# Attention: GpSimd instead of VectorE makes the low halves of the output projection's weights

## The chip, the cores and the metric

The kernel runs on one core of a Trainium2 chip. A core has five engines with a queue each, and every queue is worked off in order: PE (TensorE, matrix products; its weight loads have a row of their own, PEld), DVE (VectorE), ACT (ScalarE), POOL (GpSimd) and SP, which here only issues transfers. PE writes its products to the PSUM banks; DVE, ACT and POOL work on SBUF, DVE and ACT on PSUM too. The metric is the device time of one execution in microseconds. Three runs of the kernel before gave 622.75, 623.11 and 625.85 us; the median is 623.11.

## The reference, cut to what matters

Two layers on 256 tokens of width 1024, in float32: layer 0 mixes by pooling, layer 1 by attention with a shared K/V. Behind each stands a gated convolution FFN and a gated input embedding. The change lies in the attention of layer 1:

```
def nsa_attention(h, w_in, w_out, cos, sin, kv):
    ...
    proj = h @ w_in                       # queries and gates
    ...                                   # three branches per block of queries: compressed, selected, window
    out = gate0 * o_c + gate1 * o_s + gate2 * o_w
    ...
    o = o.transpose(1, 0, 4, 2, 3, 5).reshape(B, S, N_HEADS * HEAD_DIM)
    return o @ w_out                      # 1024 x 1024: the output projection
```

## The kernel before, in words

The products are taken in fp32r, a rounded float32. To keep float32's accuracy, each operand is split into a high part (rounded to fp32r) and a low part (what is left), and `mm3` (L103) adds three products: high by high, high by low, low by high. So every weight that comes from memory passes through three steps. `fetch` (L129) has SP load a chunk of 128 x 2048 into a `raw` buffer (three of them, used in turn). `ahead` (L138) then makes it ready in two halves of 128 x 1024: L149 on ACT casts `raw` to the high part `wh`, and L151 subtracts, `wl = raw - wh`. `wh` and `wl` have four buffers each. `take` hands the oldest finished chunk to the products and lets the next buffers be asked for.

The list `chunks` (L112 to L126) holds all chunks in the order of use. In layer 1 that is eight chunks of `wkv`, one of `wqg`, four of `wq`, four of `wout` (the output projection), and then the FFN's `wup`. A set `pooled` says which chunks have L151 on POOL (`e = G if len(made) in pooled else V`, L150). It is filled from the table `POOLED` (L44), whose numbers count from the `wqg` chunk: 0 is `wqg`, 1 to 4 are `wq`, 5 to 8 are `wout`. Before, the table is empty and DVE does all of them.

Attention (`attention_layer`) works through eight pairs of heads, by a word list (`LOOP`) that names the steps: S scores on PE (`kk`, `qq`, and a bf16 `masks` product); M the row maxima on DVE (`nm`, L810, from PSUM); E the exponentials on ACT (`pe`, L822 and L826); F and W the softmax factors and the weighting of `pe` (L833 to L849, mostly DVE); T transposes on PE (L860); P their copies to `pt` (L866 on DVE, L868 on ACT); V the values on PE (`pt`, `vv`); G the split of the result into `xo` (L945, L946). A score bank can be written again only when the maxima and exponentials of its last use are through. Between these steps the filler pieces stand: the remaining query products (`qs`), the compressed branch (`kc`, `ce`, `cst`, `spread`, `glb`), and the output projection (`xo`, L777 adds it to `x`). The tail adds the last of it (L999) and splits `x` for the FFN (`xs`, L234 on ACT, L235 on DVE).

`glb` needs words of its own: POOL clears it (L731), DVE copies into it (L733), and PE multiplies it with `w` (`w21`), the second layer of the compression of V.

Who stands where in a queue is not written out: a scheduler sets each engine's order from its own costs and from priorities. `PR` gives L149 and L151 a lower one ("w": -20), so a chunk is made ready when its engine has nothing more urgent. POOL has little else to do in attention: two memsets (L731 and L892).

Of the kernel before, what the change touches and what calls it, by code (L numbers as in the profile page):

```python
# [40 lines left out]

NROWG = 5

POOLED = ()  # L44

BANKS = ((1, 2, 3), (0, 4))

# [33 lines left out]
def body(ctx, tc, xt, xT, pT, pos, colsd, maskd, band, wpool, wup, wdn, wgate, wproj, wkv, wq, wqg, wout,  # L81
# [35 lines left out]
    for layer in range(2):  # L117
        if layer:
# [3 lines left out]
            chunks += [(wout[p, m], 8) for p in range(2) for m in range(2)]  # L122
            pooled.update(n + i for i in POOLED)
        chunks += [(wup[layer, i], KT) for i in range(NP)]
# [1041 lines left out]
```

## Time and profile before

| | before |
|---|---|
| median of the three runs | 623.11 us |
| the profiled execution, its own time | 622.48 us |
| its span, first to last instruction | 620.7 us |
| busy PE / DVE / ACT / POOL | 599.6 / 533.7 / 405.4 / 44.0 us |
| mean granted clock of PE | 0.996 |
| the chain that ended last: PE / DVE / ACT | 81% / 8% / 3% |
| L151 on DVE, whole kernel | 144 instructions, 168.5 us |

Busy time of PE includes time in which one matmul overlaps the next. The chain that ended last is followed back from the last instruction, at each step to what released it; a line that has a share there set the end, at that point. A row of the timeline gives the start, the time it took, engine, line, operation, the result and its inputs, and in brackets the idle time of the engine before it and who ended it. Consecutive instructions of the same kind are merged into one row with a count. Times of rows are microseconds from the start of the span. Attention's loop lies between 301 and 392 us; the FFN of layer 1 follows.

### The profile page before, as it was taken

The numbers are of one execution on the slowest core, as the hardware profiler recorded it, in microseconds if no ns is written. First come the engines' busy times: TensorE is split into PE (matmuls) and PEld (weight loads), VectorE is DVE, ScalarE is ACT, GpSimd is POOL, SyncE is SP. The second block draws the span as 40 slices with busy tenths as digits, with TensorE's granted clock in tenths as the row PEclk, the third lists the DMA queues.
The fourth block names the chain that finished last, engine by engine and source line by source line (L and its number), as shares of the span: only waits on it lengthen the run. The fifth ranks groups of instructions, "written<-read, shape, count | busy, mean of one in ns | idle before, by whom it ended". The sixth has DMA issues, their size and how long they took to land.

```text
span 620.7 us, 10874 instructions
## 1 busy us (share of the span) xinstructions
PE 599.6 (97%) x4134; PEld 543.2 (88%) x4134; DVE 533.7 (86%) x984; ACT 405.4 (65%) x780; POOL 44.0 (7%) x68
## 2 busy tenths in 40 slices
PE   8999999999999999999978899899999999999995
PEld 7789999999999999999865587789999999999995
DVE  3999999999888889568889975999989999888853
ACT  4986766566766658465576652877666666766643
POOL 1400000000000314000000000400000000000321
PEclk9999999999999999999998999999999999999999
DMA  8775556754454145846345023375655544552001
GB/s 332 280 261 211 204 204 223 270 205 186 187 204 153 52 140 184 303 193 178 100 138 170 2 85 119 135 273 178 229 204 190 210 176 166 193 204 102 2 2 68
DMA packets 24276, 107.31 MB, mean 173 GB/s; under 512 B 3488, under 2 KB 7456, under 8 KB 15904
## 3 DMA queue, kind: packets, MB, share of 16 engines
q1 hardware_dynamic: 23936, 105.57, 48.2%
q10 hardware_dynamic: 288, 1.05, 0.5%
q8 instruction: 32, 0.52, 0.3%
q14 instruction: 20, 0.16, 0.1%
HBM read 101.79 MB, written 1.05 MB: 166 GB/s over the span
## 4 chain that ended last, share of the span: by engine, by line
PE 81%; DVE 8%; ACT 3%; issue 2%; DMA 0%; DVEq 0%; POOLq 0%; POOL 0%; ACTq 0%
PE bank L101 79%; DVE wl L151 2%; PE bank L860 1%; DVE nm L810 1%; ACT wh L149 1%; DVE xs L235 1%; DVE dl L169 1%; DMA qq<-qp 0%; DVE rsh L595 0%; DVE un L390 0%; DVE pt L866 0%; DVE x L777 0%; DVE x L999 0%; DVE rsh L601 0%; DVE t L395 0%
## 5 line engine op out<-in xcount | busy, mean ns | idle before, releaser
L101 PE MATMUL bank<-xs,wh 128*128 128x512 f32 (+1 forms) x960 | 295.6, 365 | 1.9 <-DVE xs L235 1.9
L101 PE MATMUL bank<-xs,wl 128*128 128x256 f32 x832 | 233.3, 280 | 0.5 <-DVE wl L151 0.5
L101 PEld LDWEIGHTS bank<-xs,wh 128*128 128x128 f32 x960 | 171.8, 189 | 31.4 <-DVE xs L235 4.2
L151 DVE TENSOR_TENSOR wl<-raw,wh 128x1024 fp32r<-128x1024 f32 (+2 forms) x144 | 168.5, 1181 | 19.1 <-ACT wh L149 18.8
L149 ACT CAST wh<-raw 128x1024 fp32r<-128x1024 f32 (+2 forms) x144 | 142.3, 1008 | 40.0 <-PE bank L101 35.7
L101 PEld LDWEIGHTS bank<-xs,wl 128*128 128x128 f32 x832 | 157.4, 189 | 1.3 <-DVE wl L151 1.3
L101 PE MATMUL bank<-al,dh 128*128 128x256 f32 x352 | 99.3, 284 | 0.3 <-DVE al L404 0.3
L101 PE MATMUL bank<-ah,dl 128*128 128x256 f32 x352 | 99.0, 283 | 0.0
L101 PE MATMUL bank<-ah,dh 128*128 128x256 f32 x352 | 98.0, 284 | 0.6 <-ACT ah L403 0.4
L101 PEld LDWEIGHTS bank<-ah,dh 128*128 128x128 f32 x352 | 66.2, 190 | 2.8 <-ACT ah L403 1.2
L101 PEld LDWEIGHTS bank<-al,dh 128*128 128x128 f32 x352 | 67.4, 191 | 0.8 <-DVE al L404 0.8
L101 PEld LDWEIGHTS bank<-ah,dl 128*128 128x128 f32 x352 | 67.2, 191 | 0.0
L394 ACT ACTIVATE t<-un,cols 128x256 f32<-128x256 f32 x88 | 52.3, 602 | 12.5 <-DVE un L390 12.4
L168 ACT CAST dh<-draw 128x1024 fp32r<-128x1024 f32 x44 | 46.3, 1052 | 16.8 <-PE bank L101 16.0
L388 ACT COPY ub<-bank 128x256 f32<-128x256 f32 x88 | 31.9, 368 | 37.2 <-PE bank L101 37.2
L169 DVE TENSOR_TENSOR dl<-draw,dh 128x1024 fp32r<-128x1024 f32 x44 | 53.7, 1220 | 0.0
L395 DVE SCALAR_TENSOR_TENSOR t<-un,cols,t 128x256 f32<-128x256 f32 x88 | 41.8, 482 | 5.1 <-ACT t L394 4.7
L294 POOL TENSOR_TENSOR sqa<-sqa,sq 128x256 f32<-128x256 f32 x21 | 17.8, 845 | 376.7 <-issue 368.5
L396 DVE SCALAR_TENSOR_TENSOR t<-un,cols,t 128x256 f32<-128x256 f32 x88 | 41.9, 483 | 1.6
L389 DVE TENSOR_TENSOR ub<-bank,ub 128x256 f32<-128x256 f32 x88 | 36.6, 420 | 0.5
L390 DVE TENSOR_TENSOR un<-ub,rrow 128x256 f32<-128x256 f32 x88 | 36.5, 420 | 0.1
L399 ACT ACTIVATE sg<-t 128x256 f32<-128x256 f32 x44 | 18.4, 419 | 17.0 <-DVE t L396 14.0
(196 smaller groups left out, 857.3 us busy)
## 6 DMA issues: line engine op xcount, KB each, us to landing
raw<-in_wup SPq DMA_DIRECT2D x44, 1024.0 KB, 4.9
draw<-in_wdn SPq DMA_DIRECT2D x44, 512.0 KB, 4.8
raw<-in_wgate SPq DMA_DIRECT2D x8, 1024.0 KB, 4.8
raw<-in_wkv SPq DMA_DIRECT2D x8, 768.0 KB, 4.4
raw<-in_wq SPq DMA_DIRECT2D x4, 1024.0 KB, 5.0
raw<-in_wout SPq DMA_DIRECT2D x4, 1024.0 KB, 5.3
raw<-in_wproj SPq DMA_DIRECT2D x2, 1024.0 KB, 4.8
w<-in_cw SPq DMA_DIRECT2D x2, 1024.0 KB, 6.1
```

Of the source, the lines that this page charges most:

```text
L101: E.matmul(o, w, x, start=first, stop=last, skip_group_check=True)
L149: S.copy(hi[:, sl], raw[:, sl])
L151: e.tensor_tensor(lo[:, sl], raw[:, sl], hi[:, sl].bitcast(F32), op=ALU.subtract)
L168: S.copy(hi, raw)
L169: V.tensor_sub(lo, raw, hi.bitcast(F32))
L388: S.copy(ub, up[i][h][:, 1])
L389: V.tensor_tensor(ub, up[i][h][:, 0], ub, op=ALU.add)
L390: V.tensor_tensor(un[:, h, 2:], ub, row, op=ALU.mult)
L394: S.activation(t1, un[:, h, 2:], AF.Identity, scale=c[2], bias=c[3])
L395: V.scalar_tensor_tensor(t1, un[:, h, 1:T + 1], c[1], t1, op0=ALU.mult, op1=ALU.add)
L396: V.scalar_tensor_tensor(t1, un[:, h, 0:T], c[0], t1, op0=ALU.mult, op1=ALU.add)
L399: S.activation(sg, t[1], AF.Silu)
```

## The change

The table gets four numbers, the four `wout` chunks:

```
-POOLED = ()
+POOLED = (5, 6, 7, 8)
```

So eight instructions of L151, two for each chunk, are issued on POOL in place of DVE. ACT's casts and the loads are the same in number. The scheduler gives all engines another order from the end of the query products to the FFN. Three places of it follow, the first on POOL and PE, the second on PE, the third on DVE; rows with "+" or "-" are those that differ, and bank numbers tell the banks apart.

First place, POOL, from the last norm ahead of attention to the first instructions of the FFN:

```order
 L294 TENSOR_TENSOR sqa<-sqa,sq 128x256
 L220 TENSOR_TENSOR rcol<-ms,mhalf 128x2
+L151 TENSOR_TENSOR wl<-raw,wh 128x1024 x3
 L731 MEMSET glb 128x256
+L151 TENSOR_TENSOR wl<-raw,wh 128x1024
 L892 MEMSET spread 128x512
+L151 TENSOR_TENSOR wl<-raw,wh 128x1024 x4
 L1023 MEMSET un_4508 128x2x2
 L1023 MEMSET un_4509 128x2x2
```

The memset of `glb` now stands behind three of the subtractions, that of `spread` behind four.

First place, PE, where the first scores (bank_3384) begin; bank_3517 is the third query product:

```order
 L101 MATMUL bank_3517<-qs,wh 128x256 x2
 L101 MATMUL bank_3517<-qs,wl 128x256
-L101 MATMUL bank_3517<-qs,wh 128x256 x2
+L101 MATMUL bank_3517<-qs,wh 128x256
+L101 MATMUL bank_3390<-w_2794,glb 128x64
 L101 MATMUL bank_3384<-kk,qq 128x256 x4
 L101 LDWEIGHTS masks
```

One of the two `glb` products has moved from behind these scores to a place ahead of them.

Second place, PE, about the last pair's first scores (bank_4103); bank_4109 is the first of the output projection, bank_4036 the transposed `spread`. Before:

```order
1857 L101 MATMUL bank_4116<-kk,qq 128x512
1858 L101 LDWEIGHTS masks
1859 L101 MATMUL bank_4116<-masks 128x2x128
1860 L101 MATMUL bank_4103<-kk,qq 128x256 x4
1861 L101 LDWEIGHTS masks
1862 L101 MATMUL bank_4103<-masks 128x512
1863 L933 MATMUL bank_4036<-cols,spread 128x128 x4
```

The same place after the change:

```order
1860 L933 MATMUL bank_4036<-cols,spread 128x128 x2
1861 L101 MATMUL bank_4116<-kk,qq 128x512
1862 L101 LDWEIGHTS masks
1863 L101 MATMUL bank_4116<-masks 128x2x128
1864 L101 MATMUL bank_4109<-xo,wh 128x256 x2
1865 L101 MATMUL bank_4109<-xo,wl 128x256
1866 L101 MATMUL bank_4109<-xo,wh 128x256 x2
1867 L101 MATMUL bank_4109<-xo,wl 128x256
1868 L101 MATMUL bank_4109<-xo,wh 128x256 x2
1869 L101 MATMUL bank_4109<-xo,wl 128x256
1870 L101 MATMUL bank_4109<-xo,wh 128x256 x2
1871 L101 MATMUL bank_4109<-xo,wl 128x256
```

The scores of bank_4103 follow behind these rows: four transposes and twelve matmuls of the projection have moved ahead of them.

Third place, DVE, from the last sums of attention (L999) into the FFN of layer 1. Before:

```order
560 L999 TENSOR_TENSOR x<-bank_4462,x 128x512
561 L151 TENSOR_TENSOR wl<-raw,wh 128x1024
562 L999 TENSOR_TENSOR x<-bank_4476,x 128x512
563 L235 SCALAR_TENSOR_TENSOR xs<-x,cols,xs 128x256
564 L999 TENSOR_TENSOR x<-bank_4490,x 128x512
565 L235 SCALAR_TENSOR_TENSOR xs<-x,cols,xs 128x256 x3
566 L151 TENSOR_TENSOR wl<-raw,wh 128x1024
567 L235 SCALAR_TENSOR_TENSOR xs<-x,cols,xs 128x256 x2
568 L151 TENSOR_TENSOR wl<-raw,wh 128x1024 x2
```

The same place after the change:

```order
550 L999 TENSOR_TENSOR x<-bank_4462,x 128x512
551 L235 SCALAR_TENSOR_TENSOR xs<-x,cols,xs 128x256 x2
552 L999 TENSOR_TENSOR x<-bank_4476,x 128x512
553 L235 SCALAR_TENSOR_TENSOR xs<-x,cols,xs 128x256 x2
554 L999 TENSOR_TENSOR x<-bank_4490,x 128x512
555 L235 SCALAR_TENSOR_TENSOR xs<-x,cols,xs 128x256 x4
556 L151 TENSOR_TENSOR wl<-raw,wh 128x1024 x2
```

The two subtractions that stood between the splits of `x` are the FFN's own (`wup`, still on DVE); they have moved behind all eight splits.

## Rows read from the trace of the kernel before

**Rows 1.** The page's busy time of each engine, share of the span, instructions.

```profile
PE 599.6 (97%) x4134; PEld 543.2 (88%) x4134; DVE 533.7 (86%) x984; ACT 405.4 (65%) x780; POOL 44.0 (7%) x68
```

**Rows 2.** Busy by stretch: us, PE, PEld, DVE, ACT, POOL, PEclk, DMA share, GB/s.

```profile
301.30:391.70 90.40, 82.31 (x571) 63.28 (x570) 75.27 (x173) 54.56 (x178) 0.91 (x4) 0.98 0.31 101
329.66:334.33 4.67, 4.67 (x20) 1.80 (x20) 4.67 (x12) 3.20 (x15) 0.00 (x0) 0.76 0.73 245
343.60:347.19 3.59, 3.59 (x21) 1.35 (x21) 3.59 (x12) 2.34 (x12) 0.00 (x0) 1.00 0.01 2
...
319.00:324.00 5.00, 2.74 (x20) 2.01 (x18) 4.68 (x19) 2.94 (x5) 0.00 (x0) 1.00 0.22 52
...
391.00:399.00 8.00, 6.42 (x36) 4.91 (x35) 8.00 (x11) 6.45 (x15) 5.64 (x6) 1.00 0.20 68
```

**Rows 3.** Timeline of PE in attention: start, time, row, idle before and its releaser.

```profile
301.31 0.62 PE L101 MATMUL bank<-kk,qq 128*128 128x256 f32 x4
...
322.78 1.34 PE L860 MATMUL bank<-cols,pe 128*128 128x128 f32 x8 [2.20 <-DVE cst L919]
...
327.19 0.74 PE L101 MATMUL bank<-kk,qq 128*128 128x512 f32 x2 [1.04 <-ACT pe L826]
...
352.36 0.74 PE L101 MATMUL bank<-kk,qq 128*128 128x256 f32 x4 [1.71 <-ACT pe L822]
...
398.22 0.50 PE L101 MATMUL bank<-xs,wh 128*128 128x512 f32 x1 [1.58 <-DVE xs L235]
```

**Rows 4.** The chain that ended last, 290 to 460 us: L151's pieces.

```profile
327.27 1.14 DVE wl L151
...
390.24 1.13 DVE wl L151
...
395.54 1.76 DVE wl L151
```

**Rows 5.** DVE timeline: first and last of the eight `wout` subtractions.

```profile
296.61 1.22 DVE L151 TENSOR_TENSOR wl<-raw,wh 128x1024 fp32r<-128x1024 f32 x1
...
356.26 1.18 DVE L151 TENSOR_TENSOR wl<-raw,wh 128x1024 fp32r<-128x1024 f32 x1
```

**Rows 6.** POOL's groups by form: busy us and mean ns, then idle before.

```profile
L1048 POOL TENSOR_TENSOR sqa<-sqa,xg 128x256 f32<-128x256 f32 x5 | 3.7, 740 | 13.3 <-issue 7.3 <-ACT xg L1046 5.9
...
L731 POOL MEMSET glb<- 128x256 f32 x1 | 0.3, 312 | 24.0 <-DVE qq L610 24.0
...
L258 POOL TENSOR_SCALAR ss<-ss 128x1 f32<-128x1 f32 x1 | 0.2, 239 | 0.4 <-ACT sqs L253 0.4
```

**Rows 7.** The tile `sqa`: duration ns min/median/max, first and last start.

```profile
L294 POOL TENSOR_TENSOR sqa<-sqa,sqf x14: 731/803/1597, 20.0 to 396.3; 128x256 f32<-128x256 f32 x14
```

**Rows 8.** Timeline, 211 to 219 us: DVE's splits beside POOL's sums.

```profile
211.42 6.27 DVE L235 SCALAR_TENSOR_TENSOR xs<-x,cols,xs 128x256 fp32r<-128x256 f32 x8
...
211.40 1.62 POOL L294 TENSOR_TENSOR sqa<-sqa,sq 128x256 f32<-128x256 f32 x2 [180.81 <-issue]
...
216.39 1.90 POOL L294 TENSOR_TENSOR sqa<-sqa,sq 128x256 f32<-128x256 f32 x2 [0.27 <-ACT sq L293]
```

**Rows 9.** Line L235 by tile: duration ns min/median/max, first and last start.

```profile
L235 DVE SCALAR_TENSOR_TENSOR qs<-x,cols,qs x8: 475/477/479, 244.8 to 249.4; 128x256 fp32r<-128x256 f32 x8
```

**Rows 10.** Timeline of ACT, DVE and PE about `glb`, 297 to 307 us.

```profile
297.18 1.05 ACT L149 CAST wh<-raw 128x1024 fp32r<-128x1024 f32 x1 [2.41 <-PE bank L101]
...
305.59 0.48 DVE L733 COPY glb<-gl 128x60 f32<-128x60 f32 x4
...
306.29 0.64 PE L101 MATMUL bank<-w,glb 128*128 128x64 f32 x4
```

**Rows 11.** Timeline of SP and the page's loads: the fourth `wout` chunk.

```profile
313.19 0.61 SPq L136 DMA_DIRECT2D raw<-in_wout  x1
...
raw<-in_wout SPq DMA_DIRECT2D x4, 1024.0 KB, 5.3
```

**Rows 12.** DVE's groups by form, 300 to 362 us: the weighting of `pe`.

```profile
L842 DVE TENSOR_TENSOR pe<-pe,f 128x512 f32<-128x512 f32 x7 | 4.8, 686 | 0.0
```

## The prediction

> **What bounds the kernel now.** I read the busy times first: PE is busy for 97% of the span, DVE for 86%, POOL for 7% [rows 1]. PE is therefore the bound over the whole, and taking work off DVE can only pay where PE waits for DVE. The busy times by stretch show where that is. In attention's loop, 301.30 to 391.70, PE is busy for 82.31 of 90.40 us, so 8.1 us are idle there, while DVE works nearly without a break: 4.68 of 5.00 us from 319 to 324, 8.00 of 8.00 from 391 to 399 [rows 2]. The timeline of PE names the waits: 2.20 us at 322.78 for DVE's factors, 1.04 at 327.19 and 1.71 at 352.36 for exponentials that wait for DVE's maxima, 1.58 at 398.22 for DVE's last split of x [rows 3]. Together 6.5 us. There is one more loss: in the values product from 329.66 to 334.33 the granted clock is 0.76, and its 20 matmuls take 4.67 us, where the next one (21 rows, full clock) takes 3.59 [rows 2]. It stands right behind those waits, so 1.1 us may hang on them too. Last, the chain that ended last says how much of L151 really sets the end between 290 and 460 us: three pieces, 1.14, 1.13 and 1.76 us [rows 4]. Only the first is a `wout` subtraction; the other two are the FFN's own.
>
> **What leaves DVE.** Eight subtractions, from 296.61 to 356.26, of 1.18 to 1.23 us in their rows [rows 5]; back to back one takes 1.14 of DVE's time, as its piece on the chain shows [rows 4]. 8 x 1.14 = 9.1 us leave DVE. Seven of the eight are on no chain: DVE would have waited for PE or ACT in their place. So the 9.1 us are not the gain; the terms below are.
>
> **What it costs on POOL.** No row shows a subtraction of 128x1024 there. Two rows bound it: a sum of 128x256 takes 0.740 us, an operation on one column 0.239 [rows 6]. Four times 0.740 is 2.96; a fixed 0.24 and a slope of 0.50 us per 256 columns give 0.24 + 4 x 0.50 = 2.24, which I take, as the fixed part is seen in a row. Upwards: the longest of the sums beside busy DVE took 1.597 against 0.731 at best [rows 7], a factor of 2.2, so 4.9 us. Eight of them are 18 to 39 us on an engine with nothing else to do there.
>
> **What it takes back from DVE.** Both engines read SBUF at the same time, and rows show that this costs: eight splits of x beside POOL's sums took 6.27 us [rows 8]; alone one takes 0.477 [rows 9], so 3.8 for eight. The 2.5 us more lie beside seven sums (four rows of the timeline, of which the first and the last stand in [rows 8]): 0.35 us per sum of 256 columns. If that grows with the columns, a subtraction of 1024 stops DVE for 1.4 us. But the splits read SBUF with both inputs; the loop's maxima and copies read PSUM. I take half, 0.7 us, with bounds of 0 and 2.24 (POOL's whole operation). The Trainium skill ("SBUF — State Buffer", section "Who interferes with whom") says that a VectorE instruction with two SBUF inputs and a GpSimd instruction that reads SBUF exclude each other, and the second waits for the first to finish. By that the price would be up to 2.24 us each; the rows here show less, since eight splits and their seven sums would then have taken 3.8 + 7 x 0.74 = 9.0 us in place of 6.27. What the rule would do here is the first rival.
>
> **Place by place**, against the profiled execution's 622.48 us (span 620.7).
> A, the first scores. POOL must clear `glb` behind three subtractions, the third of which needs a cast that runs from 297.18 to 298.23 [rows 10]. 298.2 + 2.24 + 0.31 (the memset, [rows 6]) = 300.8; DVE's four copies, 0.48, end at 301.3. PE now has a `glb` product right ahead of the scores, which began at 301.31 [rows 3]; before, it came at 306.29 [rows 10]. So the new wait just fits: +0.3, bounds 0 and +2.9 (at 4.9 per subtraction 300.8 becomes 303.5, and DVE's copies slip to 304). Queued behind it on PE are the scores of the first pair, for which DVE, ACT and all later steps wait.
> B, up to the first values product (329.66). The 1.14 us at 327.27 go. In the new order the weights that PE awaits at 322.78 stand ahead of the last query's rotation, and the maximum behind the wait at 327.19 stands earlier; of these 3.24 us I take 2.0. Against that three POOL subtractions fall into the stretch where DVE is full: the loads of the third and fourth chunk come late (the fourth was issued at 313.19 and needs 5.3 us, [rows 11]), so they run between about 317 and 330. 3 x 0.7 = +2.1. Sum -1.0; bounds -4.4 and +6.7 - 1.1 = +5.6.
> C, up to the second values product: one weighting (0.69 us, [rows 12]) now comes ahead of the split of `xo`, in DVE's wait: -0.6, bounds -0.7 and 0.
> D, the wait of 1.71 at 352.36: four transposes and twelve matmuls of the projection now stand ahead of the scores that waited, and fill it: -1.2, bounds -1.7 and 0.
> E, the FFN's start: two subtractions, 1.13 and 1.76 us on the chain, move behind the last split; 2.9 us is more than PE's 1.58: -1.5, bounds -1.6 and 0. Nothing waits for them soon, since they make FFN chunks that are used two products later.
> The clock's 1.1 us I leave at 0, with -1.1 as bound. Sum: 0.3 - 1.0 - 0.6 - 1.2 - 1.5 = -4.0. C and D lie behind B in one ring of PE, DVE and ACT, and a wait that shrinks uncovers the next, so I keep -3.0. 622.48 - 3.0 = 619.5; the median of the runs lies 0.6 above the profiled execution, so I forecast 620.1, own range 617 to 621.5.
>
> **Rivals.** No gain: each POOL subtraction stops DVE for its whole 2.24 us, as the rule above has it. Then B's three cost 3 x 1.54 = 4.6 us more than I took, and 620.1 becomes 624.7; at 1.4 us each it is 622.2. For it speaks that the weighting and the rotations of the loop read SBUF with both inputs; against it, that the rows show 0.35 us per 256 columns, not 0.74. The other way to the same end is that the terms B to D do not come, as seven of the eight were hidden anyway; then only E and the 1.14 remain, less the contention: 623.1 - 2.6 + 2.1 = 622.6.
> Slower: POOL's queue becomes what PE waits for. The place is the `glb` memset behind three subtractions. At 4.9 us each PE stands for 2.9 us at the first scores, and the three in the full stretch, twice as long, stop DVE for up to 2.24 us each; with B to D lost and E kept: 623.1 + 2.9 - 1.1 + 6.7 - 1.5 = 630; with half of the stop 626.8. It decides from about 4 us per subtraction. For it speaks the row of 1.597 us; against it, that DVE in the loop also has 15 us of waits [rows 2] and reads PSUM in its maxima and copies.
> That the change does something else than it says I exclude: POOL's queue holds eight subtractions, DVE's eight fewer.
>
> **Chances.** Forecast 0.52, no gain 0.29, slower 0.17, the rest on either side 0.02. About 0.5%, 3.1 us, is what a measurement of this kernel can tell from no change, so below 620.0 is faster and above 626.2 slower. Of the forecast's 0.52, 0.42 lie below 620.0. Faster 0.43, same 0.39, slower 0.18. The range 616.5 to 625.5 takes in the forecast with part of the clock, and all of the second case; it leaves out the slower one and the best end of B.
>
> **What would show it.** On POOL eight rows of L151 of 2.2 to 3 us, the first at about 288. On PE a wait of under 1 us before the first scores with a DVE copy of `glb` as its releaser; the 1.71 us ahead of the last pair's scores gone; no wait for the last split of x. Between 317 and 330 DVE rows L842, L849, L601 and L602 longer than before, with POOL busy beside them. I would be wrong if POOL's rows took 4 us or more, if the first scores began after 303, or if the values product began later than 329.66.

## The result and the profile after

The changed kernel takes 629.43 us (median of six runs, 628.02 to 630.52), the kernel before beside it 623.16 (six runs). The ratio is 1.0097, interval 1.0077 to 1.0117: slower, by 6.3 us. The forecast was 620.1, a gain of 3.0. The profiled execution of the changed kernel has 629.8 us and a span of 628.0, 7.3 longer than that of before.

The page's busy times after, to be held against [rows 1]:

```profile
PE 603.7 (96%) x4134; PEld 547.1 (87%) x4134; DVE 537.1 (86%) x976; ACT 404.4 (64%) x780; POOL 63.7 (10%) x76
```

DVE has eight instructions fewer, worth 9.1 us, and its busy time still rose by 3.4. So other DVE rows must have grown by some 12 us. The timeline of POOL shows when it subtracts (start, time, row, idle before and its releaser; the first row is two instructions in one, the last three):

```profile
288.38 5.16 POOL L151 TENSOR_TENSOR wl<-raw,wh 128x1024 fp32r<-128x1024 f32 x2 [18.19 <-ACT wh L149]
301.97 2.40 POOL L151 TENSOR_TENSOR wl<-raw,wh 128x1024 fp32r<-128x1024 f32 x1 [8.43 <-ACT rt L597]
304.31 0.31 POOL L731 MEMSET glb<- 128x256 f32 x1
304.58 2.37 POOL L151 TENSOR_TENSOR wl<-raw,wh 128x1024 fp32r<-128x1024 f32 x1
...
325.16 2.59 POOL L151 TENSOR_TENSOR wl<-raw,wh 128x1024 fp32r<-128x1024 f32 x1 [17.74 <-ACT wh L149]
330.91 7.98 POOL L151 TENSOR_TENSOR wl<-raw,wh 128x1024 fp32r<-128x1024 f32 x3 [3.16 <-PE bank L933]
```

The timeline of DVE in the same stretches:

```profile
288.57 2.75 DVE L601 TENSOR_TENSOR rsh<-rsh,ropeS 128x512 f32<-128x512 f32 x1
291.24 2.85 DVE L608 TENSOR_TENSOR kp<-rsh,kp 128x512 fp32r<-128x512 f32 x1
...
302.12 2.33 DVE L714 TENSOR_TENSOR gt<-gt,gh 128x60 f32<-128x60 f32 x1
304.38 0.18 DVE L600 TENSOR_TENSOR rt<-bank,Cc 128x30 f32<-128x30 f32 x1
304.48 0.17 DVE L601 TENSOR_TENSOR rsh<-rsh,Cc 128x30 f32<-128x30 f32 x1
304.57 0.18 DVE L716 TENSOR_SCALAR gh<-gh 128x60 f32<-128x60 f32 x1
304.68 2.32 DVE L602 TENSOR_TENSOR rsh<-rt,rsh 128x30 f32<-128x30 f32 x1
...
325.41 2.37 DVE L833 TENSOR_SCALAR sums<-sums 128x8 f32<-128x8 f32 x1
...
331.70 0.67 DVE L600 TENSOR_TENSOR rt<-bank,ropeC 128x512 f32<-128x512 f32 x1
332.29 0.68 DVE L866 COPY pt<-bank 128x512 f32<-128x512 f32 x1
332.88 1.04 DVE L601 TENSOR_TENSOR rsh<-rsh,ropeS 128x512 f32<-128x512 f32 x1
333.85 0.68 DVE L810 TENSOR_REDUCE nm<-bank 128x2 f32<-128x512 f32 x1
334.45 2.23 DVE L602 TENSOR_TENSOR rsh<-rt,rsh 128x512 f32<-128x512 f32 x1
```

Read the two side by side. L714 on 60 columns, 0.22 us in the kernel before, starts 0.15 us after POOL's third subtraction and ends 0.08 us after it. Then POOL clears `glb` for 0.31 us, and in that gap three DVE instructions run at their usual 0.17 to 0.18. POOL's fourth subtraction starts, and L602 on 30 columns (0.18 before) ends just behind it. The width of the DVE instruction makes no difference to how long it is held. Rows that take an input from PSUM (L600, L866, L810 at 331.70 to 333.85, with POOL busy) keep their length. The four rows ahead of the first scores hold DVE 2.07, 2.16, 2.11 and 2.14 us too long, 8.5 in all; in the loop it is 2.20 (L833), 0.36, 1.55 and, in an L610 at 337.80, 0.94, 5.1 in all. 13.5 more and 9.1 less is the rise of DVE's busy time, within 1 us.

What PE sees of it, in its timeline after, against [rows 3]:

```profile
295.01 0.32 PE L688 MATMUL bank<-cols,gts 48*128 48x48 f32 x2 [1.79 <-DVE gts L686]
...
309.16 0.66 PE L101 MATMUL bank<-w,glb 128*128 128x64 f32 x2 [4.14 <-issue]
309.58 1.20 PE L101 MATMUL bank<-kk,qq 128*128 128x256 f32 x4
...
335.63 0.74 PE L101 MATMUL bank<-kk,qq 128*128 128x512 f32 x2 [2.20 <-ACT pe L826]
337.94 5.39 PE L101 MATMUL bank<-pt,vv 128*64 128x256 f32 x16 [1.44 <-DVE pt L866]
```

The first scores begin at 309.58 instead of 301.31. The first two stops reach PE as a wait of 1.79 us, for a DVE row that stands behind them; then PE stands for 4.14 us, with a `glb` product at the head of its queue. The profile names no releaser for that wait ("issue"), but DVE's copies into `glb` run from 308.59 to 309.06, and the product starts at 309.16. Behind each wait the matmuls are slow: the first scores take 1.20 us where they took 0.62, at a granted clock of 0.50 instead of 1.00. In the same way the first values product takes 5.39 us for the same 16 matmuls that took 3.88. Its granted clock is 0.51, close to the lower of the clock's two levels (1.2 and 2.4 GHz), and it stands behind waits in which PE was busy for 1.93 of 5.00 us; before, the clock was 0.71 in it (columns as in [rows 2]):

```profile
334.00:339.00 5.00, 1.93 (x9) 1.08 (x11) 5.00 (x5) 3.41 (x14) 4.89 (x2) 0.74 0.62 222
337.94:343.33 5.39, 5.39 (x18) 2.17 (x20) 5.11 (x14) 3.30 (x15) 0.95 (x1) 0.51 0.55 120
```

### The profile page after: what moved, and what is told of

The parts are those of the page before. It is cut to its first block, busy times and chain, and to the rows that moved or that the text cites. A ratio compares the mean times of both kernels' runs of the same rounds, so it can differ in the third digit from the quotient of the medians.

```text
span 628.0 us, 10862 instructions
## 1 busy us (share of the span) xinstructions
PE 603.7 (96%) x4134; PEld 547.1 (87%) x4134; DVE 537.1 (86%) x976; ACT 404.4 (64%) x780; POOL 63.7 (10%) x76
## 5 line engine op out<-in xcount | busy, mean ns | idle before, releaser
L151 DVE TENSOR_TENSOR wl<-raw,wh 128x1024 fp32r<-128x1024 f32 (+2 forms) x136 | 157.7, 1172 | 17.0 <-ACT wh L149 16.8
L168 ACT CAST dh<-draw 128x1024 fp32r<-128x1024 f32 x44 | 46.2, 1050 | 15.4 <-PE bank L101 13.5
```

The source lines that it names most:

```text
L151: e.tensor_tensor(lo[:, sl], raw[:, sl], hi[:, sl].bitcast(F32), op=ALU.subtract)
L168: S.copy(hi, raw)
```

## The experiments

Theory 1: while GpSimd runs an instruction that reads SBUF, a VectorE instruction that works on SBUF alone is held until it ends, so each subtraction costs VectorE some 2 us where such a row is next. Theory 2: the changed order, or the `glb` memset behind three subtractions, makes the loss. Each kernel ran beside the kernel before on the same chip; times are medians, and ratios have their 95% interval. In e1, e6, e9, e10, e13 and e14 PE, DVE and ACT run the changed kernel's order, instruction by instruction; in e2 they run the order of before. The marks in the table are starts in the profiled execution.

| kernel | time, us | ratio to before | first scores | first values | second values | span | DVE busy |
|---|---|---|---|---|---|---|---|
| before | 622.6 to 623.2 | 1 | 301.31 | 329.66 | 343.60 | 620.7 | 533.7 |
| after | 629.43 | 1.0097 | 309.58 | 337.94 | 353.33 | 628.0 | 537.1 |
| e1, memsets only | 618.02 | 0.992 [0.9903, 0.9936] | 302.74 | 327.98 | 341.83 | 616.5 | 526.6 |
| e2, both subtract | 632.5 | 1.0153 [1.014, 1.0166] | 301.62 | 336.83 | 353.71 | 630.9 | 543.2 |
| e3, `glb` by DVE | 629.72 | 1.011 [1.0097, 1.0123] | 309.37 | 337.52 | 353.05 | 627.7 | 538.0 |
| e4, chunks 7, 8 | 630.51 | 1.0117 [1.0103, 1.0131] | 301.69 | 338.95 | 352.29 | 629.1 | 537.7 |
| e5, chunks 5, 6 | 628.73 | 1.0088 [1.0057, 1.0118] | 309.38 | 336.48 | 351.95 | 628.7 | 538.2 |
| e9, pieces of 512 | 625.45 | 1.0048 [1.0036, 1.006] | 306.83 | 333.61 | 348.65 | 623.3 | 536.3 |
| e6, pieces of 256 | 622.58 | 0.9995 [0.9977, 1.0014] | 305.55 | 333.64 | 347.21 | 621.9 | 533.8 |
| e10, pieces of 128 | 619.9 | 0.9957 [0.9945, 0.9969] | 303.07 | 329.03 | 343.22 | 617.9 | 532.2 |
| e13, pieces of 64 | 620.31 | 0.9954 [0.9937, 0.997] | 302.96 | 327.07 | 343.51 | 618.2 | 528.5 |
| e14, copies | 617.39 | 0.9905 [0.9887, 0.9922] | 303.06 | 326.99 | 341.45 | 616.1 | 527.9 |

**e1, GpSimd writes but does not read.**

```
-                    e = G if len(made) in pooled else V
-                    e.tensor_tensor(lo[:, sl], raw[:, sl], hi[:, sl].bitcast(F32), op=ALU.subtract)
+                    e = (lambda o, a, b, op: [G.memset(o.bitcast(F32), 0.0) for _ in range(2)]) if len(made) in pooled else V.tensor_tensor
+                    e(lo[:, sl], raw[:, sl], hi[:, sl].bitcast(F32), op=ALU.subtract)
```

> The changed kernel with each of GpSimd's eight subtractions replaced by two memsets of the same half tile: GpSimd only writes, and reads nothing from SBUF. It leaves out the low parts of the output projection's weights (zeros stand there). The order of TensorE, VectorE and ScalarE is the changed kernel's, instruction by instruction, and GpSimd's queue is as long and stands in the same places. Theory 1 (while GpSimd reads two SBUF tiles, a VectorE instruction that works on SBUF alone stands still until GpSimd's instruction ends): no VectorE instruction is stretched to 2 us any more, the first scores begin near 302 instead of 309.58 on the trace, and the time is 618 to 621 us. Theory 2 (the new order, or the zeroing of glb behind three subtractions in GpSimd's queue): nothing of that has changed, 627 to 630 us.

618.02 us, 11.4 less than the changed kernel in the same order. Theory 2 falls: the new order, with DVE relieved but without the reads, is 0.8% faster than before. The same DVE rows, beside POOL's first four memsets (287.40 to 291.03), in the timeline of this kernel:

```profile
288.61 0.68 DVE L601 TENSOR_TENSOR rsh<-rsh,ropeS 128x512 f32<-128x512 f32 x1
289.86 0.69 DVE L608 TENSOR_TENSOR kp<-rsh,kp 128x512 fp32r<-128x512 f32 x1 [0.57 <-ACT kp L606]
...
297.73 0.98 DVE L713 TENSOR_SCALAR gt<-gt 128x60 f32<-128x60 f32 x1
...
301.28 1.03 DVE L733 COPY glb<-gl 128x60 f32<-128x60 f32 x4
...
319.55 0.93 DVE L849 TENSOR_SCALAR pe<-pe,f 128x256 f32<-128x256 f32 x1
```

The rows with two SBUF inputs keep 0.68 and 0.69. Rows that read and write one tile do not: the weighting L849 takes 0.93 instead of its 0.35 beside memsets from 319.38 on, L713 takes 0.98 instead of 0.19 beside those from 297.71 on, and the four copies into `glb` 1.03 instead of 0.48. So writes hold another kind of DVE instruction. Two of these rows, L713 and L733, stand on the way to the first scores, so e1 is not wholly free of stops: part of the 1.4 us by which its first scores come later than before is theirs.

**e2, both engines subtract.**

```
-                    e = G if len(made) in pooled else V
-                    e.tensor_tensor(lo[:, sl], raw[:, sl], hi[:, sl].bitcast(F32), op=ALU.subtract)
+                    for e in (V, G) if len(made) in pooled else (V,):
+                        e.tensor_tensor(lo[:, sl], raw[:, sl], hi[:, sl].bitcast(F32), op=ALU.subtract)
```

> The kernel before, VectorE keeping all its subtractions, and GpSimd making the same eight low parts over again right behind VectorE's (the same values into the same tiles). The order of TensorE, VectorE and ScalarE is the kernel before's, instruction by instruction. Theory 1 (GpSimd's reads stop VectorE): eight stops of about 2.1 us are added and nothing is taken from VectorE, four of them ahead of the first scores; 628 to 634 us. Theory 2 (the new order): the order is the old one, 623 to 625 us.

632.5 us, inside theory 1's range and far from theory 2's. With the order of before, the first scores come on time (no `glb` product stands ahead of them), but the first values are 7.2 us late. So the reads cost about as much in either order: 9.5 us over before here, and 11.4 in the new order (after against e1).

**e3, no queue on POOL for `glb`.**

```
-                G.memset(glb, 0.0)
+                V.memset(glb, 0.0)
```

> The changed kernel with the zeroing of glb on VectorE instead of GpSimd, so that nothing that the compressed keys need stands behind the subtractions in GpSimd's queue. Theory 1 (VectorE stands still during the subtractions): the stops ahead of the first scores remain, 628 to 630 us. Theory 2, in the form that the queue of GpSimd delays the chain of glb: the chain is free of it, first scores some 3 to 4 us earlier, 625 to 626 us.

629.72 us, first scores at 309.37 (here all `glb` products stand ahead of them). POOL's queue was not what the chain of `glb` waited for; DVE itself stood still.

**e4 and e5, half of the chunks each** (`POOLED = (7, 8)` and `POOLED = (5, 6)`).

> Only the third and fourth of the four weight chunks on GpSimd (four subtractions, all inside the attention loop); the first two are VectorE's as before. Theory 1 (stops of VectorE cost what stands on the path there; four stops ahead of the first scores made the loss): first scores as before, the two waits that VectorE's subtractions made in the loop and at the feed-forward part's start shorter by some 2 to 3 us together, one values product later by 1.5 us: 620 to 623 us. Rival (a stop costs its 2 us wherever it stands): 626 to 628 us.

> Only the first and second of the four weight chunks on GpSimd: its four subtractions fall ahead of and around the first scores, none inside the loop. Theory 1 (a stop of VectorE costs its length wherever VectorE is the engine that TensorE waits for, and stops that hit the same slack overlap, so the losses of the two halves do not add up to that of the whole): first scores some 8 us late as with all four chunks on GpSimd, and no more than 2 us of it made up in the loop; 628 to 632 us. Rival (the losses add up: all four 629.4, the loop's two alone 630.5, before 623.2, so the first two alone are worth -1 us): 621 to 623 us.

Here my own theory of the place fell: e4 was expected at 620 to 623 us and took 630.51; e5, at 628.73, came inside its range. I took the four stops ahead of the first scores for the loss and those of the loop for nearly free, since the stretch from the first scores to the first values had not grown (28.35 us before, 28.36 after). But by the ratios the loop's two chunks alone cost 7.3 us (6.4 to 8.2), the first two alone 5.5 (3.5 to 7.3), and all four 6.0 (4.8 to 7.3). In e4 POOL subtracts at 311.86 to 317.18 and 325.62 to 330.81, ahead of the first values. Its DVE and PE timelines:

```profile
312.11 2.88 DVE L602 TENSOR_TENSOR rsh<-rt,rsh 128x512 f32<-128x512 f32 x1
314.91 2.95 DVE L849 TENSOR_SCALAR pe<-pe,f 128x256 f32<-128x256 f32 x3
...
326.34 1.66 DVE L836 TENSOR_TENSOR f<-f,gate 128x8 f32<-128x8 f32 x1
...
328.86 2.50 DVE L842 TENSOR_TENSOR pe<-pe,f 128x512 f32<-128x512 f32 x1
```

```profile
317.39 0.66 PE L860 MATMUL bank<-cols,pe 128*128 128x128 f32 x4 [1.92 <-DVE pe L849]
...
331.50 2.24 PE L860 MATMUL bank<-cols,pe 128*128 128x128 f32 x9 [5.20 <-DVE cst L919]
```

They hit the weighting of `pe` (L842, L849) and its factors (L836), which PE's transposes wait for, and PE stands 1.92 and 5.20 us. In the changed kernel the stops of the loop fell on L833, L601, L602 and L610, and the stretch to the first values, which e1 does in 25.24 us, took 3.1 us more than there; that it looked unchanged against before is relief and stops cancelling. So a stop costs where DVE is what PE waits for, in the loop as ahead of it, and the losses of the halves do not add up. Why they add up to so little more than either alone I did not settle beyond that.

**e9, e6, e10 and e13, the subtraction cut into pieces** of 512, 256, 128 and 64 columns. Here the edit for 128:

```
-                    e = G if len(made) in pooled else V
-                    e.tensor_tensor(lo[:, sl], raw[:, sl], hi[:, sl].bitcast(F32), op=ALU.subtract)
+                    for q in [slice(j, j + 128) for j in range(sl.start, sl.stop, 128)] if len(made) in pooled else [sl]:
+                        (G if len(made) in pooled else V).tensor_tensor(lo[:, q], raw[:, q], hi[:, q].bitcast(F32), op=ALU.subtract)
```

> The changed kernel with each of GpSimd's eight subtractions cut into four of 256 columns: the same reads and sums, 32 instructions. Theory 1a (GpSimd has the shared SBUF port for one instruction at a time, and VectorE gets in between two): a stopped VectorE instruction is held for a quarter of the time, under 0.7 us instead of 2.1 to 2.4, and GpSimd waits for VectorE in turn; first scores 303 to 306 instead of 309.58; 622 to 627 us. Theory 1b (VectorE stands for as long as GpSimd has subtractions queued): stops of 2 us and over remain, 628 to 631 us.

> The changed kernel with each of GpSimd's subtractions cut into two of 512 columns; the order of TensorE, VectorE and ScalarE stays the changed kernel's, instruction by instruction, as it does with pieces of 256. Theory 1a (a VectorE instruction is held until the one GpSimd instruction that has the port ends): the loss falls with the length of one GpSimd instruction, stops of about 1.2 us, and the time lies between whole subtractions (629.4) and pieces of 256 (622.6): 625 to 627.5 us. Rival (what helped with pieces of 256 was another thing, such as the later start of GpSimd's queue): 622 to 623 or 629 to 630 us.

> The same with pieces of 128 columns, 64 instructions. Theory 1a: stops of 0.3 us and less; between pieces of 256 (622.6) and no reads at all (618.0), less what GpSimd's own cost for each instruction adds: 619.5 to 622 us. Rival (GpSimd's cost for each instruction, or a fixed cost of handing the port over, sets a floor): 622.5 to 625 us.

> The changed kernel with each of GpSimd's subtractions cut into sixteen of 64 columns, 128 instructions, everything else in the same order. Theory 1a with a cost for each instruction: the time so far falls by about 3 us for each halving (629.4, 625.5, 622.6, 619.9); stops would shrink to some 0.2 us, but GpSimd's busy time for one chunk grows (16 pieces of 128 columns took 8.3 us beside VectorE): 618.5 to 620.5 us. Rival (each handing over of the port costs VectorE a fixed time, so that more pieces cost more): 621 to 624 us.

Same reads, same sums, same order, and the time falls with the length of a piece: 629.4, 625.5, 622.6, 619.9, then 620.3. All four came inside theory 1a's ranges. With pieces of 128 the rows of before and after can be compared once more, in the DVE timeline of e10 beside POOL's pieces from 287.85 and from 298.17 on:

```profile
288.04 0.82 DVE L601 TENSOR_TENSOR rsh<-rsh,ropeS 128x512 f32<-128x512 f32 x1
...
298.31 0.40 DVE L714 TENSOR_TENSOR gt<-gt,gh 128x60 f32<-128x60 f32 x1
...
298.94 0.44 DVE L602 TENSOR_TENSOR rsh<-rt,rsh 128x30 f32<-128x30 f32 x1
```

L714 takes 0.40 instead of 2.33, L602 0.44 instead of 2.32: held for a piece, then let in. GpSimd is busy for longer. Its groups from 284 to 345 us, in e10 and in e13:

```profile
L151 POOL TENSOR_TENSOR wl<-raw,wh 128x128 fp32r<-128x128 f32 x64 | 33.7, 562 | 30.5 <-ACT wh L149 30.3 <-ACT rt L597 0.2
```

```profile
L151 POOL TENSOR_TENSOR wl<-raw,wh 128x64 fp32r<-128x64 f32 x128 | 45.1, 389 | 22.7 <-ACT wh L149 22.7
```

With 64 columns GpSimd is busy 45.1 us for what took it 20.5 whole (5.16 + 2.40 + 2.37 + 2.59 + 7.98). Most of that comes with the number of instructions, not with being held: the shortest of the 128 pieces takes 0.31 us, and 128 x 0.31 is already 40 us. Nothing more is gained, though DVE's busy time falls further. PE's timelines show where the lead goes, in e10 and in e13:

```profile
329.03 2.80 PE L101 MATMUL bank<-pt,vv 128*64 128x256 f32 x16
```

```profile
327.07 4.49 PE L101 MATMUL bank<-pt,vv 128*64 128x256 f32 x16
...
338.12 1.26 PE L101 MATMUL bank<-kc,qq 128*128 128x32 f32 x10 [1.84 <-DMA qq<-qp]
```

With 64 columns the first values come 1.96 us earlier, but that product then takes 1.69 us longer (granted clock 0.62 instead of 1.00, behind a wait of 1.92 us), and PE stands 1.84 us for a transfer of `qq`; the second values come 0.29 us later than in e10. Why the slow clock and the wait come just there is not settled.

Pieces of 128 columns beat both kernels: 619.9 us, 0.43% under before (interval 0.31 to 0.55%), 9.5 us under the change as made. That is under the 0.5% which I called the limit of one measurement, but the interval excludes no change.

**e14, one read instead of two.**

```
-                    e = G if len(made) in pooled else V
-                    e.tensor_tensor(lo[:, sl], raw[:, sl], hi[:, sl].bitcast(F32), op=ALU.subtract)
+                    e = (lambda o, a, b, op: G.tensor_copy(o, b)) if len(made) in pooled else V.tensor_tensor
+                    e(lo[:, sl], raw[:, sl], hi[:, sl].bitcast(F32), op=ALU.subtract)
```

> The changed kernel with each of GpSimd's eight subtractions replaced by a copy of the high part into the low part's tile: GpSimd reads one SBUF tile instead of two, and writes as before; the output projection's low parts are wrong (the high part stands in them). The order of the other engines is unchanged. If any read of GpSimd holds VectorE's instructions with two SBUF inputs: they stand still as long as the copy lasts (a copy needs no more than the 2.4 us of a subtraction, and no less than the 0.95 us of a memset), 622 to 629 us. If it takes both reads of a subtraction: as with memsets alone, 617 to 619.5 us.

By the time, 617.39, this agrees with the second reading; by the trace, with the first. POOL's copies at 288.00 to 290.49 and at 298.31 (1.04 us) and DVE beside them, in its timeline:

```profile
288.19 1.39 DVE L601 TENSOR_TENSOR rsh<-rsh,ropeS 128x512 f32<-128x512 f32 x1
289.50 1.52 DVE L608 TENSOR_TENSOR kp<-rsh,kp 128x512 fp32r<-128x512 f32 x1
...
298.46 0.95 DVE L714 TENSOR_TENSOR gt<-gt,gh 128x60 f32<-128x60 f32 x1
```

One read is enough to hold DVE until the copy's end: 1.52 instead of 0.69, 0.95 instead of 0.22. But a copy lasts 1.04 to 1.51 us (eight copies, median 1.12), and stops of 0.8 us and less cost hardly anything here: the first scores come at 303.06, 0.3 later than without reads. My range for that case priced the stops as if all of them lay on the path; that DVE had the time to spare is the likely reason, not one that a run shows by itself.

**e11, pieces of 256 for chunks 7 and 8 alone, and e12, pieces of 256 with `glb` cleared by DVE.**

> Only the third and fourth chunk on GpSimd, in pieces of 256 columns; the first two are VectorE's. Ahead of the first scores nothing is held. Theory 1a: the loop's whole subtractions cost 7.3 us over before; in pieces this falls to about a quarter, and the work taken from VectorE in the loop is gained: 621 to 623.5 us. Rival (in the loop VectorE is the engine that TensorE waits for, so that 16 pieces hold it as long as 4 whole ones): 626 to 630 us.

> All four chunks on GpSimd in pieces of 256 columns, and the zeroing of glb on VectorE. With whole subtractions that zeroing made no difference (629.7 against 629.4), since VectorE stood still anyway. Theory 1a: with short stops the queue of GpSimd is what the chain of glb waits for, first scores 1 to 2 us earlier than with pieces alone: 620 to 622 us. Rival (the chain waits for VectorE still): 622 to 623.5 us.

e11: 624.56 us (1.0036 [1.0021, 1.005]), between the two ranges and a little slower than before; by the ratios it costs 2.2 us where whole subtractions in the loop cost 7.3. e12: 622.36 (1.0005 [0.9994, 1.0016]), in the rival's range and no different from e6, so POOL's queue is not the limit with short stops either.

**e7 and e8, order alone.** `'w': -20` becomes -40 and -80 in the priorities, all subtractions on VectorE.

> The kernel before, all subtractions on VectorE, with the scheduler's lead for the weight splits set from -20 to -40, so that casts and subtractions give way to more of the attention's work. If the gain that the changed order has without GpSimd's reads (618.0 us against 623.2) lies in what VectorE does ahead of its subtractions, some of it comes back here: 620 to 622.5 us. If it lies in the 9 us of subtractions that VectorE no longer has to do, order alone gives nothing: 623 to 625 us.

> As the run before with the lead at -80: the splits give way still more. If order alone gives part of the gain: 619.5 to 622.5 us. If the gain lies in the work that VectorE no longer has to do: 623 to 627 us, later than with -40, since the low parts then come last and the output projection waits for them.

622.55 (0.9998 [0.9981, 1.0016]) and 623.53 (1.0007 [0.9992, 1.0022]): no difference either way; the first lies between its two ranges, the second in the range for order that gives nothing. With these two priorities order alone gives nothing; that another order would is not excluded.

## Why the prediction was wrong

The direction was wrong, and one step did it: **What it takes back from DVE**, the stop of 0.7 us for each POOL subtraction. It was 2.07 to 2.20 us in five of the eight and 0.36 to 1.55 in the other three, wherever a DVE row with SBUF inputs was next. The derivation went wrong in two places. The 0.35 us per sum came from [rows 8], where eight splits ran beside seven sums of 256 columns. That is an average, and I scaled it with the columns as if reads were slowed, though what happens is that one instruction is held to the end of the other. The rows of before show it once the eight splits are taken one by one, and not as one merged row (line L235 from 211 to 218 us, duration in ns as minimum, median and maximum):

```profile
L235 DVE SCALAR_TENSOR_TENSOR xs<-x,cols,xs x8: 471/962/1014, 211.4 to 216.7; 128x256 fp32r<-128x256 f32 x8
```

Six of the eight take 0.96 to 1.01 us and two 0.47, as much as alone. A held split is thus 0.48 to 0.54 us longer, beside sums of 0.74 to 1.01 us. And I then halved it because many rows of the loop read PSUM. Those rows do keep their length, but the next row with SBUF inputs is held for what is left of the subtraction, so PSUM rows only shorten a stop (0.36 and 1.55 us in the loop), they don't halve the price of the rest. The rule that I cited and set aside (the Trainium skill, "SBUF — State Buffer", section "Who interferes with whom") was right: the traces agree, with L714 at 2.33 us beside a subtraction of 2.40, and in e1 rows with two SBUF inputs at 0.68 beside memsets. My argument against it, that the splits would then have taken 9.0 us, assumed that each of the seven sums stops a split for its whole length; six splits were held, and each for some 0.25 us less than a sum of 0.74.

The second part of the same failure is where I charged it. Term A counted only POOL's queue, not one stop, though four of the eight subtractions run between 288 and 307, on DVE's way to the first scores. The on-record rival with the full stop, "no gain", charged three stops only and ended at 624.7 at most: it left the four ahead of the first scores out as well. The "slower" rival had the right sign and reached 626.8 to 630, but by a subtraction of over 4 us and a queue on POOL; the subtractions took 2.37 to 2.82 us, and e3 shows the queue to be worth nothing.

Term by term, with e1 as the run in which order and relief of DVE act without the reads; each stretch is a difference of two marks in the table:

| term | forecast | e1 | after | reads (after - e1) |
|---|---|---|---|---|
| A, to the first scores | +0.3 | +1.4 | +8.3 | +6.8 |
| B, to the first values | -1.0 (-3.1 without stops) | -3.1 | 0.0 | +3.1 |
| C, to the second values | -0.6 | -0.1 | +1.5 | +1.5 |
| D and E, to the end | -2.7 | -2.4 | -2.4 | 0.0 |
| span | -4.0, kept -3.0 (-6.1 without stops, kept -5.1) | -4.2 | +7.3 | +11.5 |

So the gains were about right in sum: without stops I would have kept -5.1, and without the reads the change gives -4.2 us on the span (-5.2 by the medians). Term by term they were less exact: A came 1.1 us dearer, some of it by the memsets' own stops, and C's 0.6 hardly came. What failed is the last column, for which I had +2.1 in B alone; it measured 11.5, of which 6.8 in A. C is the slow clock behind the waits: 5.39 us for a values product that takes 3.89 in e1. D and E came close to the forecast: the 1.71 and the 1.58 us of [rows 3] have no counterpart after. (Of the 6.5 us of waits that the prediction set against the loop's 8.1 idle us, that 1.58 at 398.22 lies behind the loop; no term hangs on it.)

POOL's subtraction, taken as 2.24 us from [rows 6], took 2.37 to 2.82 (line L151 on POOL after, columns as above):

```profile
L151 POOL TENSOR_TENSOR wl<-raw,wh x8: 2372/2530/2820, 288.4 to 336.1; 128x1024 fp32r<-128x1024 f32 x8
```

Of the things to look for, the first subtraction at about 288 came true, and of the long DVE rows beside POOL L601 and L602 were right, L842 and L849 wrong. Of the three conditions that I set for being wrong two came true, first scores after 303 and values after 329.66; no subtraction took 4 us.

## What to carry to other kernels

Before work goes from VectorE to GpSimd, ask what VectorE's next instructions read: in these traces a row with both inputs in SBUF (and some with one) stood until GpSimd's instruction ended, whatever its own size, so the price of a stop is nearly the length of GpSimd's instruction and not a share of it. Count every place where such a row is next on the way to what TensorE waits for. Read merged rows one by one: an average over held and free rows hides the stop. If the work must go there, cut it into short instructions: here pieces of 128 columns turned +6.3 us into -2.7, while pieces of 64 brought no more. And a run in which GpSimd only writes, in the same order, tells the gain of the relief and the price of the reads apart in one go, but for the rows that its writes hold.

## What was not expected of the hardware

A DVE instruction of 30 columns took 2.32 us beside a GpSimd subtraction, one of 8 columns with a single tile in (L833) 2.37. A single read by GpSimd holds two-input rows just as two do (e14). Memsets on GpSimd left the two-input rows L601 and L608 at their length but held rows with one tile in and one out: `TENSOR_SCALAR` L849, 0.93 instead of 0.35, and L713, 0.98 instead of 0.19 (e1). Cutting costs GpSimd time: 128 pieces of 64 columns kept it busy for 45.1 us, the whole subtractions for 20.5.
